# Batched matrix product, 32 x (256x512 by 512x384): half a y batch loaded ahead of the first x, and the first store issued by ScalarE

## Chip, cores, metric

One core of a Trainium2 chip. The time is in device microseconds (us) of one execution; before has a median of 136.12 us over the six runs that were made beside the changed kernel (135.89 to 136.56). GB/s counts what the core's 16 DMA engines moved.

## The reference

```python
# x: (32, 256, 512) float32, y: (32, 512, 384) float32
return np.einsum('bij,bjk->bik', x, y).astype(np.float32)
```

The inputs are 41.94 MB, the output 12.58 MB.

## The kernel before

Everything is recorded in program order. x comes in eight loads of four batches (2 MB, 16 KB to a partition), y in 32 loads of one batch (768 KB, 6 KB to a partition; a unit u is two batches, so two "halves"), the result leaves in 16 stores of 768 KB. All go through SyncE (`nc.sync`). TensorE transposes x, VectorE and ScalarE cast transposes and y to fp16, TensorE multiplies, VectorE and ScalarE copy the products to `o_sb`.

```python
    def load(u):
        if u == 0:
            load_x(0)
        if (u + 1) * G % Q == 0 and u + 1 < U:
            load_x((u + 1) * G // Q)
        y_of[u] = y_pool.tile([P, G, NJ, K], F32, name="y_sb")      # 5 buffers
        for g in range(G):                                          # the two halves
            keep(nc.sync.dma_start(out=y_of[u][:, g],
                    in_=y[u * G + g].rearrange("(q t) k -> q t k", q=P)))
    ...
    def store(u):
        keep(nc.sync.dma_start(
                out=out[u * G : (u + 1) * G].rearrange("g (m e) k -> (g m) e k", e=NE),
                in_=o_of.pop(u)))
    ...
    ahead = LAG - 2                     # 2
    for u in range(ahead):
        load(u)
    for s in range(U + 2):
        if s + ahead < U:
            load(s + ahead)
        ...                             # transpose, collect(s-2), multiply(s-1), round_y(s)
        if s >= 2:
            store(s - 2)
```

The recording layer gives the transfers eight completion semaphores in turn, so a transfer is issued only when the one eight places earlier has landed.

## Time and profile before

| What | Value |
|---|---|
| median, six runs | 136.12 us |
| span in the profile | 134.3 us |
| bytes through the DMA engines | 54.65 MB, mean 407 GB/s |
| from 5 to 129 us | about 423 GB/s |
| TensorE / VectorE / ScalarE busy | 66 / 42 / 48% |

The prediction below shows the lines of the page, of the stretches and of SyncE's issues, and reads them. The columns are the stretch, its length, then for each engine its busy us (instructions), then the granted clock, the DMA share and GB/s.

### The profile page before, as it was taken

The numbers are of one execution on the slowest core, as the hardware profiler recorded it, in microseconds if no ns is written. First come the engines' busy times: TensorE is split into PE (matmuls) and PEld (weight loads), VectorE is DVE, ScalarE is ACT, GpSimd is POOL, SyncE is SP. The second block draws the span as 40 slices with busy tenths as digits, with TensorE's granted clock in tenths as the row PEclk, the third lists the DMA queues.
The fourth block names the chain that finished last, engine by engine and source line by source line (L and its number), as shares of the span: only waits on it lengthen the run. The fifth ranks groups of instructions, "written<-read, shape, count | busy, mean of one in ns | idle before, by whom it ended". The sixth has DMA issues, their size and how long they took to land.

```text
span 134.3 us, 1968 instructions
## 1 busy us (share of the span) xinstructions
PE 88.5 (66%) x768; PEld 73.2 (55%) x768; DVE 56.2 (42%) x128; ACT 63.9 (48%) x129; POOL 0.7 (1%) x6
## 2 busy tenths in 40 slices
PE   0049494979299767786099771976439986597920
PEld 0049474768177666666078661864427665476810
DVE  0004717471743365711634318460363425628620
ACT  3004837662762476712744428560475336738610
POOL 2000000000000000000000000000000000000000
PEclk9999999999959999999968999999965899779997
DMA  5999999999999999999999999999999999999993
GB/s 112 415 400 450 409 417 421 456 388 421 417 448 408 409 428 421 457 394 417 413 443 436 408 417 428 442 422 402 425 423 444 426 402 427 419 427 419 417 394 158
DMA packets 8073, 54.65 MB, mean 407 GB/s; under 512 B 896, under 2 KB 896, under 8 KB 7040
## 3 DMA queue, kind: packets, MB, share of 16 engines
q1 hardware_dynamic: 8064, 54.53, 97.8%
q8 instruction: 6, 0.10, 0.3%
q14 instruction: 3, 0.02, 0.0%
HBM read 41.94 MB, written 12.58 MB: 406 GB/s over the span
## 4 chain that ended last, share of the span: by engine, by line
DMA 78%; PE 13%; ACT 4%; DVE 0%; issue 0%
DMA y_sb<-in_y_dram 40%; DMA x_sb<-in_x_dram 38%; PE o_ps L130 9%; PE t_ps L99 3%; ACT xt_sb L107 2%; ACT y_r L116 1%; ACT o_sb L143 1%; DVE o_sb L145 0%
## 5 line engine op out<-in xcount | busy, mean ns | idle before, releaser
L130 PE MATMUL o_ps<-y_r,xt_sb 128*64 128x384 f16 x512 | 52.4, 364 | 28.5 <-ACT o_sb L143 20.8
L130 PEld LDWEIGHTS <-xt_sb 128*64 128x64 f16 x512 | 39.1, 121 | 38.8 <-issue 22.4
L116 ACT CAST y_r<-y_sb 128x384 f16<-128x384 f32 x64 | 29.5, 514 | 38.7 <-DMA y_sb<-in_y_dram 38.6
L99 PE MATMUL t_ps<-identity,x_sb 128*128 128x128 f32 x256 | 36.9, 301 | 11.4 <-DMA x_sb<-in_x_dram 11.4
L99 PEld LDWEIGHTS t_ps<-identity,x_sb 128*128 128x128 f32 x256 | 34.1, 211 | 16.0 <-issue 16.0
L118 DVE CAST y_r<-y_sb 128x384 f16<-128x384 f32 x64 | 20.0, 356 | 46.7 <-DMA y_sb<-in_y_dram 46.7
L107 ACT CAST xt_sb<-t_ps 128x512 f16<-128x512 f32 x32 | 22.4, 731 | 23.6 <-PE t_ps L99 23.6
L105 DVE CAST xt_sb<-t_ps 128x512 f16<-128x512 f32 x32 | 22.6, 728 | 24.1 <-PE t_ps L99 23.8
L145 DVE COPY o_sb<-o_ps 128x384 f32<-128x384 f32 x32 | 16.3, 544 | 2.1 <-PE o_ps L130 2.1
L143 ACT COPY o_sb<-o_ps 128x384 f32<-128x384 f32 x32 | 13.9, 492 | 1.3 <-PE o_ps L130 1.3
L107 ACT ACT_TABLE_LOAD x1 | 1.3, 1283 | 0.7 <-PEq L192 0.7
masks.py:199 POOL TENSOR_SCALAR_AFFINE_SELECT identity<-identity 128x128 f32<-128x128 f32 x1 | 0.3, 294 | 0.1
masks.py:197 POOL MEMSET identity<- 128x128 f32 x1 | 0.2, 206 | 0.3 <-POOLq L192 0.3
L192 POOL MEMSET const-bfloat16-1.0<- 128x1 bf16 x1 | 0.1, 102 | 0.0
L192 POOL MEMSET const-uint8-127<- 128x1 uint8 x1 | 0.1, 102 | 0.0
L192 POOL MEMSET const-float32-0.0<- 128x1 f32 x1 | 0.1, 99 | 0.2 <-issue 0.2
L192 POOL MEMSET const-float32-1.0<- 128x1 f32 x1 | 0.1, 99 | 0.0
## 6 DMA issues: line engine op xcount, KB each, us to landing
y_sb<-in_y_dram SPq DMA_DIRECT2D x32, 768.0 KB, 17.9
x_sb<-in_x_dram SPq DMA_DIRECT2D x8, 2048.0 KB, 20.8
out_dram<-o_sb SPq DMA_DIRECT2D x16, 768.0 KB, 17.8
```

Of the source, the lines that this page charges most:

```text
L99: nc.tensor.transpose(t_ps[:, f, h], x_sb[:, h * NE + e + f, t::NJ], identity)
L105: keep(nc.vector.tensor_copy(dst, t_ps))
L107: keep(nc.scalar.copy(dst, t_ps))
L116: keep(nc.scalar.copy(yr_of[u][:, g, t], y_sb[:, g, t]))
L118: keep(nc.vector.tensor_copy(yr_of[u][:, g, t], y_sb[:, g, t]))
L130: nc.tensor.matmul(o_ps[g * M : (g + 1) * M], xt_sb[:, t, e, a * PQ : (a + 1) * PQ].rearrange("c p h -> c (p h)"), y_r[:, g, t], start=(t ...
L143: keep(nc.scalar.copy(o_of[u][:, e], ps_of[u][e]))
L145: keep(nc.vector.tensor_copy(o_of[u][:, e], ps_of[u][e]))
L192: nc = _bacc.Bacc("TRN2", target_bir_lowering=False, num_devices=1)
```

## The change

The intent: let a small transfer fill the DMA engines first, and take the first store, which waits for compute, out of the row of loads that SyncE issues, so that it runs beside them.

```diff
     def load(u):
-        if u == 0:
-            load_x(0)
 ...
+            if u == 0 and g == 0:
+                load_x(0)
 ...
     def store(u):
+        queue = nc.scalar if u == 0 else nc.sync
         keep(
-            nc.sync.dma_start(
+            queue.dma_start(
```

## The prediction

> **What bounds the kernel now.** I read the page first: busy shares (part 1), then the slices of the span (part 2), to see whether an average hides stages.
>
> ```profile
> PE 88.5 (66%) x768; PEld 73.2 (55%) x768; DVE 56.2 (42%) x128; ACT 63.9 (48%) x129; POOL 0.7 (1%) x6
> ...
> PEclk9999999999959999999968999999965899779997
> DMA  5999999999999999999999999999999999999993
> ...
> DMA packets 8073, 54.65 MB, mean 407 GB/s; under 512 B 896, under 2 KB 896, under 8 KB 7040
> ```
>
> No compute engine is above 66%, while the DMA row is full in every slice but the first and the last. So the 54.65 MB that pass the 16 DMA engines set the time, and only the filling and the draining of that stream can be shortened. To size these two I took the stretch view (the last two columns are the DMA share and GB/s; before them the granted clock).
>
> ```profile
> 0.00:5.00 5.00, 0.00 (x0) 0.00 (x0) 0.00 (x0) 1.28 (x1) 0.70 (x6) 1.00 0.67 203
> 5.00:112.00 107.00, 75.64 (x651) 63.00 (x652) 46.47 (x106) 52.17 (x106) 0.00 (x0) 0.94 1.01 423
> 112.00:124.00 12.00, 8.44 (x69) 6.73 (x69) 6.94 (x16) 7.45 (x17) 0.00 (x0) 0.86 1.02 424
> 124.00:129.00 5.00, 4.41 (x55) 3.49 (x50) 2.77 (x6) 3.01 (x8) 0.00 (x0) 1.00 1.02 419
> 129.00:134.30 5.30, 0.00 (x0) 0.00 (x0) 0.00 (x0) 0.00 (x0) 0.00 (x0) 0.85 0.56 231
> ```
>
> From 5 to 129 us the DMA engines never pause: 423 GB/s, share about 1. The first 5 us move 5 x 203 = 1015 KB, worth 2.4 us at 423 GB/s, so the fill costs 2.6 us. The last 5.3 us move 5.3 x 231 = 1224 KB, worth 2.9 us, so the drain costs 2.4 us. Together 5.0 us of 134.3 us, most of it latency of the first and the last transfer. A gain of 2% (2.7 us) would have to remove over half of that.
>
> Next, whether SyncE, which issues every transfer, ever lets the stream run dry. The view of its issues (start, duration, what):
>
> ```profile
> 0.74 0.38 SPq L66 DMA_DIRECT2D x_sb<-in_x_dram  x1
> 1.17 0.89 SPq L81 DMA_DIRECT2D y_sb<-in_y_dram  x2
> 2.11 0.63 SPq L66 DMA_DIRECT2D x_sb<-in_x_dram  x1
> 2.78 2.04 SPq L81 DMA_DIRECT2D y_sb<-in_y_dram  x4
> 8.60 0.33 SPq L66 DMA_DIRECT2D x_sb<-in_x_dram  x1
> 10.48 9.00 SPq L81 DMA_DIRECT2D y_sb<-in_y_dram  x4
> 23.92 0.35 SPq L150 DMA_DIRECT2D out_dram<-o_sb  x1
> 24.37 0.39 SPq L66 DMA_DIRECT2D x_sb<-in_x_dram  x1
> ```
>
> By 4.8 us eight transfers are out. From there each issue waits for the transfer eight places earlier (the order of instructions shows eight completion semaphores used in turn), so some seven or eight transfers are always queued. The page's issues say what that means: 17.9 us from issue to landing for a y half batch whose 768 KB are worth 786 / 423 = 1.86 us.
>
> ```profile
> y_sb<-in_y_dram SPq DMA_DIRECT2D x32, 768.0 KB, 17.9
> x_sb<-in_x_dram SPq DMA_DIRECT2D x8, 2048.0 KB, 20.8
> out_dram<-o_sb SPq DMA_DIRECT2D x16, 768.0 KB, 17.8
> ```
>
> SyncE's list of waits names the wait that the change goes after:
>
> ```profile
> SPq L150 <- DVE o_sb L145: 20.3, 5, 7.1
> ```
>
> Before the first store SyncE stands 4.3 us (19.5 to 23.9) waiting for o_sb, and the next loads stand behind it. But with about 16 us of queued transfers in hand, these 4.3 us never reach the DMA engines: slices 6 and 7 run at 421 and 456 GB/s.
>
> **What the Trainium skill says.** "DMA: Bandwidth & Descriptors", section "Issuing engines are not separate DMA queues": transfers of scalar and sync run on the same 16 engines, and another issuer saves only the sequencer's time to initiate. The trace has 0.34 us for such an issue, and SyncE has idle time for it. Same page, "Queues, rings and completion order": each DMA engine takes turns, packet by packet, between the queue rows that have work. So a store on ScalarE's row overtakes queued loads, but each of its packets takes a load packet's place. No trace yet shows it, as all data here are on one queue. Same page, "Where 436 GB/s comes from": the fabric's ceiling is 435 GB/s; this trace's 423 is 97% of it, so the middle holds no rate to win.
>
> **The change part by part.** No instruction is removed and no byte. ScalarE gets one more issue, SyncE one fewer.
>
> (a) y first. Before, x0 landed at 8.60 us (SyncE's release) and the first y half at 10.48. Changed, that y half is first. By 1.86 us per half, x0 should land near 10.5 and the half near 8.60 - 4.96 + 1.86 = 5.5 (x0's 2.1 MB are worth 4.96 us). The second half and x1 keep their places (about 12.3 and 17.3). The sum of the stream is unchanged: 0 us on the DMA path. Compute pays: the first transposes need x0 and move from 8.72 to about 10.6, finishing at 16.6 in place of 14.72. The first products finish at about 21.5 in place of 19.58, all following work up to 1.9 us later. This lies beside the stream: through about 30 us it releases nothing that the DMA lacks (x buffers: the fourth x reuses the first, whose transposes end at 16.6, and it is not issued before 22.9).
>
> (b) The fill. Rows of x are 16 KB to a partition and rows of y 6 KB; smaller first packets could complete a little earlier. I give this -0.1 us, a guess within the 2.6 us of fill.
>
> (c) The store on ScalarE. In the order of instructions it stands behind the two casts of the second half of x1. Before, these two started at 27.55 and 28.51 and took 0.73 to 0.75 us, so ended near 29.3; with (a) near 31. So the first store is issued about 7 us later than before (23.92), not earlier. It then shares the engines half and half with y loads: 2 x 1.86 = 3.7 us plus about 2 us of latency, landing near 37, before it was 40.0. The y halves queued in that time land up to 1.86 us later; x3, behind the store before, still lands near 45, since the same bytes precede it. Sum for the stream: 0. ScalarE loses 0.35 us once; it is 48% busy, and waits for y casts a total of 38.6 us. 0 on the path.
>
> (d) SyncE no longer stands at 19.5 to 23.9: the next x load goes out at about 22.9 in place of 24.37. It joins a queue with over 10 us of work, so 0.
>
> (e) The end. After the last y half lands (the last casts by VectorE start at 124.15), five stores remain in both kernels: 5 x 1.86 = 9.3 us, to 133.45, just where the last one lands (129.07 issue + 4.4). The order of instructions from the second store on is the same, so this end is the same length. The last store's issue is also set by compute, nearly level with the queue: the share dips to 0.54 at 129.5.
>
> Sum: 136.2 - 0.1, so 136.1 us.
>
> **The rivals.** First: compute, started 1.9 us later, stays late and carries this into the last store. For it: the chain of waits has a stretch of PE work at the end, and queue and compute are level there. Against it: PE is 66% busy, stands 20.8 us before products in total, and DVE and ACT wait for y 46.7 and 38.6 us; the delay is eaten within the first few batches. Worth at most +1.9, 138.1 us.
>
> Second: the start really was slow because x came first, and small packets fill the engines sooner. For it: 2.6 us of fill, share 0.64 between 2 and 3 us. Against it: the issue at 0.74 and its latency are the same for any first transfer. Up to -0.8, 135.4 us.
>
> Third: two queues alternating between reads and writes cost rate. For it: x, y and store packets of different size then share an engine. Against it: only one store of sixteen. 10% of rate lost over 3.7 us would be +0.4, 136.6 us.
>
> Fourth: the granted clock drops during the last products. It was 0.5 from 116 to 119 us, where 32 products took 4.47 us against 2.79 at full clock. On the last 64 that is +3.4 us, 139.6. Against it: nothing in the change touches it, and three runs of before stay within 0.4%.
>
> **Range and chances.** Runs of before spread 136.05 to 136.56. With fill -0.8 and shared queues or late compute +0.8 about 136.1, the range is 135.3 to 137.0. Faster by 2% needs 133.5, over half of fill and drain: 3%. Slower by 2% needs 138.9, which only the throttled end or compute late throughout could bring: 3%. Within: 94%.
>
> **What would show it.** Right: share about 1.0 and about 423 GB/s from 5 to 129 us again; fill and drain within 0.5 us of 2.6 and 2.4; first transposes at about 10.6; the first store issued by ACT at about 31, landing in some 6 us where others take 17.8; the last y casts still near 124. Wrong: a stretch in the middle with a share below 0.9 (the stream ran dry, or two queues clash), a fill changed by over 1 us, or compute gaps that push the last store's issue beyond 130.

## More of the kernel before

```profile
28.00:40.00 12.00, 8.47 (x74) 6.79 (x75) 6.19 (x15) 7.29 (x16) 0.00 (x0) 0.88 1.02 423
```

The stream of transfers runs through it at its usual 423 GB/s.

## The result, and the profile after

The changed kernel takes 136.54 us (median of six runs, 136.06 to 136.71); before, 136.12. The ratio is 1.0024, with a 95% interval of 0.9999 to 1.0049. A ratio here is the mean time of one kernel's fast runs over that of the other's fast runs of the same rounds, so it is not quite the ratio of the medians. Whether the changed kernel is 0.2% slower at all is on the edge of what six runs can show. The profiled run of the changed kernel happens to be its fastest (136.06 us, span 134.3), so its trace understates the difference.

SyncE's and ScalarE's issues in the changed kernel (start, duration, what; from the timeline up to 42 us):

```profile
0.74 0.38 SPq L79 DMA_DIRECT2D y_sb<-in_y_dram  x1
...
5.23 0.33 SPq L66 DMA_DIRECT2D x_sb<-in_x_dram  x1
10.14 10.85 SPq L79 DMA_DIRECT2D y_sb<-in_y_dram  x4
...
22.63 0.33 SPq L66 DMA_DIRECT2D x_sb<-in_x_dram  x1
...
29.30 0.37 ACTq L152 DMA_DIRECT2D out_dram<-o_sb  x1
```

An issue is also a clock for landings, since it waits for one. At 5.23 us the first y half has landed, and at 10.14 us x0 has. Before, the same two transfers, in the other order, were both down at 10.48: the same bytes came 0.34 us sooner. SyncE is no longer held from 19.5 to 23.9 us. The first store is issued at 29.30 us instead of 23.92, because it stands behind ScalarE's casts of the transposes; the prediction put it at about 31.

The page's issues say how long that store was under way:

```profile
out_dram<-o_sb SPq DMA_DIRECT2D x15, 768.0 KB, 17.8
out_dram<-o_sb ACTq DMA_DIRECT2D x1, 768.0 KB, 8.7
```

So it does overtake queued loads: 8.7 us against 17.8. The stretches, read against those of before:

```profile
0.00:5.00 5.00, 0.00 (x0) 0.00 (x0) 0.00 (x0) 1.28 (x1) 0.70 (x6) 1.00 0.68 252
5.00:112.00 107.00, 77.32 (x656) 64.06 (x657) 46.71 (x106) 52.24 (x106) 0.00 (x0) 0.92 1.01 420
...
129.00:134.30 5.30, 0.00 (x0) 0.00 (x0) 0.00 (x0) 0.00 (x0) 0.00 (x0) 0.65 0.60 247
```

The first 5 us move 252 GB/s instead of 203: 245 KB more, worth 0.58 us at 423 GB/s by this count, or 0.34 us by the landings. (The window counts a packet whole when it starts; the two counts need not agree, and I go by the landings.) The fill did get shorter. But the middle falls from 423 to 420 GB/s: over 107 us that is 107 x 3 / 423 = 0.76 us lost. Cutting the middle finer finds the loss in one place:

```profile
28.00:40.00 12.00, 8.78 (x82) 7.38 (x83) 6.52 (x16) 7.23 (x15) 0.00 (x0) 0.93 1.02 393
```

393 GB/s instead of 423 over 12 us: 12 x 30 / 423 = 0.85 us. The DMA share stays at 1.02. The share counts the time that packets take, so a stretch in which each packet takes longer looks just as full; only GB/s shows it. Eight tenths lost and a third won leave +0.5 us, in the range of the measured +0.24% (0.33 us). In this one trace, the fastest run, less of it is left: the last y cast starts at 124.31 us instead of 124.15, and the span is the same. In this trace it is also where the first store shares the engines with loads, so the suspicion falls on the second queue first.

### The profile page after: what moved, and what is told of

Read it like the earlier page. It is cut to its first block, busy times and chain, and to the rows that moved or that the text cites. A ratio compares the mean times of both kernels' runs of the same rounds, so it can differ in the third digit from the quotient of the medians.

```text
span 134.3 us, 1969 instructions
## 1 busy us (share of the span) xinstructions
PE 89.2 (66%) x768; PEld 73.4 (55%) x768; DVE 56.5 (42%) x128; ACT 64.1 (48%) x129; POOL 0.7 (1%) x6
## 4 chain that ended last, share of the span: by engine, by line
DMA 78%; PE 13%; ACT 4%; DVE 0%; issue 0%
DMA y_sb<-in_y_dram 44%; DMA x_sb<-in_x_dram 34%; PE o_ps L130 9%; PE t_ps L99 3%; ACT xt_sb L107 2%; ACT y_r L116 1%; ACT o_sb L143 1%; DVE o_sb L145 0%
## 5 line engine op out<-in xcount | busy, mean ns | idle before, releaser
L130 PE MATMUL o_ps<-y_r,xt_sb 128*64 128x384 f16 x512 | 53.3, 368 | 27.7 <-ACT o_sb L143 20.0
L116 ACT CAST y_r<-y_sb 128x384 f16<-128x384 f32 x64 | 29.3, 512 | 36.6 <-DMA y_sb<-in_y_dram 36.6
## 6 DMA issues: line engine op xcount, KB each, us to landing
out_dram<-o_sb SPq DMA_DIRECT2D x15, 768.0 KB, 17.8
```

The lines of the kernel that those rows point to most:

```text
L116: keep(nc.scalar.copy(yr_of[u][:, g, t], y_sb[:, g, t]))
L130: nc.tensor.matmul(o_ps[g * M : (g + 1) * M], xt_sb[:, t, e, a * PQ : (a + 1) * PQ].rearrange("c p h -> c (p h)"), y_r[:, g, t], start=(t ...
```

## The experiments

The theory that I began with (A): y first shortens the fill, and the store on ScalarE's queue slows the engines while two queues are served. Rivals: B, scatter only; C, compute starts 1.5 us later and that costs. The first four kernels ran on one chip, each in six runs beside eleven of before (136.12 us).

### y first alone

```diff
-        queue = nc.scalar if u == 0 else nc.sync      # of the changed kernel
+        queue = nc.sync
```

> Only the first part of the change: the first y half ahead of the first x; all stores on SyncE. Theory A (two small effects that cancel: the fill gets 0.35 us shorter, the store on ScalarE's queue costs 0.5 to 0.8 us by slowing the DMA engines while both queues are served): 0.3 us faster than before, about 135.8 us; the last y casts begin at about 123.8 in place of 124.15; no stretch between 5 and 129 us below 410 GB/s. Rival B (the 0.4 us between the medians is scatter of the runs, neither part does anything): equal to before within 0.1 us. Rival C (the later x, so later compute, is what costs): slower than before by 0.3 us or so, as after is.

Measured: 136.94 us, ratio 1.0048 (1.0028 to 1.0069). A miss for theory A: slower, not faster. The stretches:

```profile
0.00:5.00 5.00, 0.00 (x0) 0.00 (x0) 0.00 (x0) 1.28 (x1) 0.70 (x6) 1.00 0.66 252
...
30.00:36.00 6.00, 4.76 (x48) 4.08 (x45) 2.54 (x7) 3.14 (x8) 0.00 (x0) 1.00 1.03 357
```

The fill is shorter here too, and the slow stretch is here without any second queue: 357 GB/s where before has 421. From 28 to 40 us it is 384, a loss of 12 x 39 / 423 = 1.1 us. Less 0.4 us of fill (x0 is down at 10.09), that is 0.7 us; the medians differ by 0.8 (the profile fell on the slowest of the six runs, 137.12 us).

### The store on ScalarE alone

```diff
+        queue = nc.scalar if u == 0 else nc.sync      # against before
         keep(
-            nc.sync.dma_start(
+            queue.dma_start(
```

> Only the second part: x first as before, the first store on ScalarE. Theory A: 0.5 to 0.8 us slower than before, about 136.7 us; the 6 us after that store's issue run at about 365 GB/s in place of 421, and the last y casts begin at about 124.7. Rival B: equal to before within 0.1 us. Rival C: equal to before, since x comes first again.

Measured: 136.14 us, ratio 1.0006 (0.9985 to 1.0026). Theory A has fallen: this part costs nothing that can be seen. The store lands in 8.1 us, so it shared the engines, and the stretch is full:

```profile
30.00:36.00 6.00, 4.08 (x41) 3.49 (x37) 0.63 (x2) 0.93 (x2) 0.00 (x0) 1.00 1.01 414
```

### Eight stores on ScalarE

```diff
+        queue = nc.scalar if u < 8 else nc.sync
```

> x first as before, the first eight stores on ScalarE instead of one. Theory A with a cost for each store that shares the engines with loads: 8 times 0.5 to 0.8 us, so 140 to 142.5 us. Rival A2 (a cost once, of waking the second queue or of its first use): about 136.7 us. Rival B: 136.1 us.

Measured: 136.03 us, ratio 0.9993 (0.9977 to 1.0010). Even eight such stores cost nothing. The page's issue line and the stretches:

```profile
out_dram<-o_sb ACTq DMA_DIRECT2D x8, 768.0 KB, 9.8
```

```profile
30.00:36.00 6.00, 4.47 (x46) 3.71 (x41) 0.63 (x2) 1.11 (x3) 0.00 (x0) 1.00 1.02 411
36.00:112.00 76.00, 53.11 (x468) 42.83 (x469) 34.53 (x80) 38.24 (x79) 0.00 (x0) 0.91 1.01 424
```

The stores land in 9.8 us instead of 17.8, and the rate stays at 424 GB/s. Stores that overtake loads neither win nor lose, as every byte that goes earlier makes another go later.

### Eight loads on ScalarE

```diff
+            queue = nc.scalar if g == 1 and 3 <= u < 11 else nc.sync
             keep(
-                nc.sync.dma_start(
+                queue.dma_start(
```

> All stores on SyncE, x first, but eight of the 768 KB loads (second halves of y 3 to 10) on ScalarE's queue. It tells what about the second queue costs. If any two queues in turn cost rate: slower by about as much as with eight stores on ScalarE. If it is stores and loads in turn on one DMA engine that cost (reads and writes of HBM mixed packet by packet): within 0.3 us of before, so 136 us. If ScalarE's stalls before an issue matter: gaps in PE and a DMA share below 0.9.

Measured: 136.14 us, ratio 1.0000 (0.9983 to 1.0017). Two queues with loads cost nothing either. That was to tell apart mechanisms of a cost which the other runs show not to exist.

So the cost belongs to y first. Is it late compute (C), or do the transfers themselves run slower (D)? The next four kernels ran on another chip, each in five runs beside nine of before (136.01 us).

### Late compute, loads as before

```diff
+        if q == 0 and half == 0:
+            for i in range(8):          # eight dummy transposes of x0, never read
+                if i % 4 == 0:
+                    t_ps = tpsum_pool.tile([P, 2, H, Q * PQ], F32, name="t_ps")
+                keep(nc.tensor.transpose(t_ps[:, i // 2 % 2, i % 2], x_sb[:, i, 0::NJ], identity))
```

> Loads and stores exactly as before (x first, all on SyncE); only the first transposes are held up by eight dummy transposes of x0 whose result is never read, about 1.6 us, as long as y first held them up. Theory C (y first costs because compute starts later): about 0.8 us slower, 136.9 us. Theory D (y first shortens the fill but brings a stretch of slow DMA packets at about 34 us that costs more; compute plays no part): equal to before within 0.2 us, 136.1, and no 3 us stretch below 380 GB/s between 5 and 128 us.

Measured: 136.07 us, ratio 1.0005 (0.9978 to 1.0031). The timeline shows the delay (1.95 us of dummies ahead of the real transposes), and the rate does not suffer:

```profile
8.90 1.95 PE L97 MATMUL t_ps<-identity,x_sb 128*128 128x128 f32 x8 [8.90 <-DMA x_sb<-in_x_dram]
10.65 5.00 PE L108 MATMUL t_ps<-identity,x_sb 128*128 128x128 f32 x32
```

From 28 to 40 us it has 421 GB/s. Theory C has fallen: transposes that start 1.9 us later, as late as with y first or later, cost nothing that the medians show. The trace has the delay shrinking: the products of the second unit start at 23.80 us against 23.56 before.

### Both y halves first

```diff
-            if u == 0 and g == 0:       # of y first alone
+            if u == 0 and g == 1:
                 load_x(0)
```

> Both halves of the first y ahead of the first x, stores on SyncE. Theory D in its plain form (it is y first that brings the slow stretch): about 137, with a stretch below 330 GB/s between 28 and 40 us. Theory C: x lands 1.86 us later still, so slower again than y first alone, about 137.7. Theory E (the slow stretch depends on how the 16 DMA engines happen to be offset against one another, and any order may or may not bring it): no such rule; the first landing is early (about 4.5 us) and the time is anything from 135.7 to 137.

Measured: 136.78 us, ratio 1.0052 (1.0022 to 1.0082), with 400 GB/s from 28 to 40 us (370 from 30 to 36). Transposes now start at 12.18 us, 2 us later than with one half first, and the time is no worse; so C fails here too. The slow stretch is there again.

### x first, in two transfers

```diff
-        keep(nc.sync.dma_start(out=x_of[q], in_=x[...].rearrange(...)))
+        parts = 2 if q == 0 else 1
+        for k in range(parts):          # 8 KB rows instead of 16 KB for the first x
+            rows = slice(k * R // parts, (k + 1) * R // parts)
+            keep(nc.sync.dma_start(out=x_of[q][:, rows], in_=x[...].rearrange(...)[:, rows]))
```

> x first, but the first x in two transfers of 8 KB rows in place of one of 16 KB rows. If the 0.4 us of fill that y first gains is due to smaller packets at the start: x0 lands at about 8.2 to 8.4 in place of 8.6 and the time is 135.8 if nothing slow follows. Theory D: no slow stretch, since x is first. Theory E: it may come here too. If neither: 136.1.

Measured: 136.78 us, ratio 1.0043 (1.0020 to 1.0065). x0 lands at about 8.5 us, hardly sooner than 8.60. There is a weak slow stretch (412 GB/s from 28 to 40 us, 0.3 us lost), and the time is 0.7 us longer than before. The stretch accounts for less than half of that. In the one trace there is, the rest comes from the end. First before, then this run:

```profile
115.54 4.47 PE L130 MATMUL o_ps<-y_r,xt_sb 128*64 128x384 f16 x32 [2.69 <-ACT o_sb L143]
```

```profile
115.77 5.33 PE L133 MATMUL o_ps<-y_r,xt_sb 128*64 128x384 f16 x32 [3.65 <-ACT o_sb L146]
```

The granted clock is 0.50 from 115 to 121 us (before, 0.72 over the same time), and the last products start at 124.08 us instead of 123.01. The last y casts no longer wait for their load, so here compute, and not the stream, sets the end. The profiled run of late compute, the slowest of its five (136.77 us), has the same 5.33 us. Whether the other runs of x in two lose their time in this way, no profile shows.

### y first, and y cast first

```diff
         if s == 0:
+            round_y(0)                  # ahead of the transposes
             transpose(0, 0)
             transpose(0, 1)
 ...
-        if s < U:
+        if 0 < s < U:
             round_y(s)
```

> As y first alone, but ScalarE and VectorE cast the first y before they empty the first transposes, so that compute catches up part of its delay: first products start at about 16 us, as before, in place of 17.3. Theory C: most of the 0.8 us comes back, about 136.3 us. Theory D: still about 136.9, with the slow stretch at 31 to 37 us in the trace. Theory E: anything between, with or without the stretch, and the time follows the stretch.

Measured: 136.72 us, ratio 1.0046 (1.0022 to 1.0070). Products start at 15.88 us, as early as before (15.91), and nothing comes back. The stretch is there: 385 GB/s from 28 to 40 us. Of the theories C and D, D stands.

What brings it? One concrete candidate (F) was that y first lets SyncE queue the third x at 5.23 us instead of 8.60, because the first transfer lands so early. The other question was whether compute has a hand in it at all. Three kernels on a third chip, beside nine runs of before (136.06 us).

### y first, the third x held back

```diff
         x_of[q] = x_pool.tile([P, R, J], F32, name="x_sb")
+        if q == 2:                      # waits for the first x to land
+            keep(nc.gpsimd.tensor_copy(x_of[2][:, 0, 0:1], x_of[0][:, 0, 0:1]))
```

> As y first alone, but the third x may not be issued before the first x has landed (a one-element copy on GpSimd between their tiles), so at about 10.1 us in place of 5.2; before issues it at 8.6. Theory F (y first queues the 2 MB of the third x too early, and that is what brings the slow packets at 31 to 37 us): no slow stretch, the 0.4 us of fill stay won, 135.7 us. Theory D without F: still about 136.8, slow stretch as before.

Measured: 136.95 us, ratio 1.0061 (1.0033 to 1.0089). The third x is issued at 10.31 us, as meant, and the stretch is still there:

```profile
10.31 0.33 SPq L68 DMA_DIRECT2D x_sb<-in_x_dram  x1
```

```profile
28.00:40.00 12.00, 8.84 (x79) 7.23 (x80) 6.11 (x16) 7.09 (x15) 0.00 (x0) 0.89 1.01 394
```

Theory F has fallen.

### Transfers alone, y first and x first

Both kernels: no compute, and every store writes one tile of zeros. Their outputs are wrong, which doesn't matter for the times. Loads and stores stand in the order of y first alone, and of before.

```diff
+    zero = const_pool.tile([P, NE, K], F32, name="zero")
+    keep(nc.gpsimd.memset(zero, 0.0))
     for s in range(U + 2):
         if s + ahead < U:
             load(s + ahead)
-        ...                             # transpose, collect, multiply, round_y
         if s >= 2:
+            o_of[s - 2] = zero
             store(s - 2)
```

> Wrong result on purpose: all loads and stores of y first alone in the same order, no compute at all; the stores write a tile of zeros. If the slow stretch is between the DMA engines and HBM alone: it is here too, 0.5 to 1 us lost between 28 and 40 us. If it takes compute (engines reading SBUF while DMA writes it, or the first store's wait): no stretch, about 423 GB/s throughout. The time without the compute behind the last load is about 133 to 134 us either way.

> Wrong result on purpose: the same without compute with x first, the control. No slow stretch expected. If the stretch is DMA and HBM alone, this is 0.3 to 0.8 us faster than the y first one; if it takes compute, it is 0.3 to 0.4 us slower than the y first one (the fill alone).

Measured: y first 135.29 us, x first 135.31 us (ratios to before 0.9949 and 0.9943). They tie. First y first, then x first:

```profile
28.00:40.00 12.00, 0.00 (x0) 1.00 1.02 404
```

```profile
28.00:40.00 12.00, 0.00 (x0) 1.00 1.02 423
```

With no instruction on any compute engine from 28 to 40 us the slow stretch is there with y first (a loss of 12 x 19 / 423 = 0.54 us) and absent with x first. So it arises between the DMA engines and the memories, and compute is not needed for it. The earlier fill (x0 down at 10.06 us against 10.43 for the same bytes) pays for most of it, hence the tie: the expectation of a difference of 0.3 to 0.8 us was a miss, and so was the time of 133 to 134 us (only the spans, 133.5 us, lie there). The two numbers also say what compute costs at most in these two orders: transfers alone take 135.3 us, so before stands only 0.8 us (0.6%) above them.

### y first, its first piece a quarter

```diff
+            cuts = [0, 1, NJ] if u == 0 and g == 0 else [0, NJ]
+            for a, b in zip(cuts, cuts[1:]):
-                out=y_of[u][:, g], in_=y[u * G + g].rearrange(...)
+                out=y_of[u][:, g, a:b], in_=y[u * G + g].rearrange(...)[:, a:b]
```

> As y first alone, but its first half y comes as two transfers, a quarter (1.5 KB rows) and the rest (4.5 KB rows). It shifts the DMA engines against one another at the start and keeps the order of the bytes. If the slow stretch follows from the order of the loads (y first): it is here too, 0.6 to 1.1 us between 28 and 40 us, and the time is 136.5 to 137. If it follows from a chance offset of the engines: it may be gone, and then the fill's 0.4 us make this the fastest version, about 135.7 us.

This kernel ran on the first chip again, in six runs beside eleven of before (136.09 us). Measured: 137.46 us (136.37 to 138.09), ratio 1.0100 (1.0071 to 1.0130): the slowest of all, and the most scattered. Its profile fell on its fastest run:

```profile
28.00:40.00 12.00, 8.78 (x82) 7.47 (x83) 6.93 (x16) 7.73 (x16) 0.00 (x0) 0.94 1.02 420
```

420 GB/s: this one execution has no slow stretch, though a y load comes first. It paid at the start instead: the first y half and x0 were down at 10.8 us, later than the same bytes in before (10.48). What its runs of 138 us did, no profile shows. So "y first brings the stretch" is not a rule; a small shift at the start can make it vanish in one execution. That speaks for a dependence on how the 16 engines stand against one another (theory E), but does not show it. Theory E in its simplest form, the wider apart the worse, does not fit: for the transfer that lands between 34 and 35 us, as the stretch begins, the first and the last of the 16 engines are 0.8 us apart in the transfers alone with y first (slow stretch), and 1.6 us in before (none).

### The packets themselves

The trace has each DMA packet with its duration. Counting the 6 KB packets (y loads and stores) that started from 28 to 40 us, one execution of each kernel (some traces fell on a slow run, as y first alone at 137.12 us, some on the fastest, as y cast first at 136.36):

```
kernel                     packets  median ns  over 300 ns  longest ns
before                        640      236           0         248
store on ScalarE              640      234          10         499
eight stores on ScalarE       641      234          13         608
eight loads on ScalarE        596      235           5         654
late compute                  640      236           6         456
transfers alone, x first      640      236           8         436
x in two                      639      235          19         627
y first, a quarter            639      235           8         435
changed kernel                640      234          71         648
y first alone                 628      235          58        1234
both y halves first           637      235          49        1189
y first, y cast first         638      234          59         913
y first, third x late         630      235          48        1369
transfers alone, y first      637      236          43         694
```

The median packet is the same everywhere, 234 to 236 ns. The six kernels in which a whole y half comes first have 43 to 71 slow packets in these 12 us; the six with an undivided x first have 0 to 13.

One suspect is in all fourteen kernels and was never taken out: the first store. The slow packets come shortly before it or as it begins. In the changed kernel most lie between 31.2 and 34.0 us, and the store's own packets, on ScalarE's queue, start at 33.09; with the store on ScalarE alone, 31.4 to 32.1 and 31.91; with eight stores there, 31.9 to 33.1 and 32.29. In the y first kernels with all stores on SyncE most lie between 33.4 and 36.6 us, and the store lands at 39.5 to 41.6. So a store that comes earlier goes with slow packets that come earlier, whichever load is first. In the changed kernel all 71 are on SyncE's queue, so they are loads, and none of the store's own is slow. That the first store brings them, and y first only makes them many, is a rival that no run tests: it would take a kernel whose first store comes later, or that has none.

## Why the prediction was right

- **The bound, and the total.** It put the change at 136.1 us within 135.3 to 137.0, "within 2%"; measured 136.54. The argument held: bytes through the DMA engines set the time, and the change removes none. The transfers alone, at 135.3 us, confirm it independently.
- **(a) y first.** Predicted: first y half down at 5.5 us, x0 near 10.5, transposes at about 10.6, first products done at about 21.5. Measured: 5.22, 10.14, 10.26 and 21.00. The differences are the fill's gain. That the compute delay does not reach the end was right, and the late compute kernel shows it (1.0005).
- **(b) The fill.** Predicted -0.1 us, called a guess; measured -0.34 us by landings. The direction was right and the size too small; the truth lies between the guess and the second rival's bound of -0.8.
- **(c) The store on ScalarE.** Issued at 29.30 us (about 31 predicted), under way 8.7 us (about 6 predicted), so down at 38 us; a net of 0 for the stream is what that part alone measured (1.0006), and eight of them too (0.9993). The third rival, a loss of rate with two queues, had the trace of the changed kernel on its side and was still wrong: the same loss is there with one queue and absent with two queues and x first.
- **(d) SyncE's wait.** The next x load went out at 22.63 us (22.9 predicted) and gained nothing, as said.
- **(e) The end.** Both profiled spans are 134.3 us. The fourth rival, a lower clock in the last products, did not come in this trace (the last 64 take 5.39 us, as before); what a low clock just before them costs is seen in x in two.
- **The step that failed** is "0 us on the DMA path" in (a). The prediction expected "about 423 GB/s from 5 to 129 us again". With y first, 6 KB packets turn slow at some 31 to 37 us and cost 0.5 to 1.1 us in the six traces that have it. This term was missing; it and the fill are of opposite sign, so the total came out within the range. A right total here is partly the luck of two small terms.
- The prediction's own sign of being wrong, "a share below 0.9", could not have found it: the share stayed at 1.02.

What stays open: why loads that begin with y meet slow packets 30 us later. Shown not to be needed: a second queue, late compute, an early third x, compute of any kind. Not shown either way: the part of the first store. Also open is the extra time of x in two transfers, which one trace alone puts down to the end, and of the quarter piece, of which no profile shows a part. Whether the two parts of the change together cost less than y first alone (1.0024 against 1.0048) can't be told: the intervals overlap, and they ran in different rounds. No version with a right result ran faster than before beyond the noise.

## What to carry to other kernels

Here the DMA engines were full from start to end, and moving issues to another engine or another place won nothing. In such a case measure the transfers alone first, as that time is the floor for their order (here 135.3 of 136.1 us). Look for losses in GB/s, not in the DMA share: here slow packets kept it at 1.02. And when a trace shows a loss beside a suspect, test the suspect alone: moving the store to the second queue, which the changed kernel's trace accused, cost nothing by itself (1.0006).

## What the Trainium skill lacked or had wrong

- "DMA: Bandwidth & Descriptors", section "Queues, rings and completion order", says that each DMA engine takes turns between the queue rows that have work. The runs agree (a store on ScalarE's row lands in 8.1 to 9.8 us, where SyncE's take 17.8) and add what it doesn't say: taking turns costs no rate (eight stores 0.9993 of the time of before, eight loads 1.0000).
- No page has the slow stretch: with the same bytes in a slightly different order at the start, 6 KB packets that take 234 ns took up to 1369 ns at about 31 to 37 us, with 384 to 400 GB/s in place of 423 over 12 us in the five kernels with compute, and 404 with none.
- No page says that fetching instructions shows in a bulk stream; it would belong to "Runtime: NRT & Kernel Launch", section "Instruction fetch mechanics". The profile page of before lists 6 packets, 0.10 MB, of instructions on a queue of their own. As the first of them passes, at 27.3 us, the 16 engines' landings of one transfer spread from 0.6 us to 1.6 us and stay apart; with the transfers alone, x first, there are no such packets, and the spread is still 0.9 us there. That the packet is the cause is argued from this coincidence, not tested.
